# A two-layer attention and pooling trunk on one core: another order of column blocks, longer leads for weights, and w_ada's half tiles from the 33rd on issued by GpSimd

## The chip, the core and the metric

The kernel runs on one core of a Trainium2 chip. It is one program for five engines: TensorE (PE: matmuls and transposes; its weight loads are a row of their own, PEld), VectorE (DVE), ScalarE (ACT), GpSimd (POOL) and SyncE (SP). Here SP issues nearly all transfers between HBM and on-chip memory. Each engine carries out its instructions in the order in which the program wrote them, and each waits by itself for what its next instruction needs. The metric is the device time of one execution in microseconds (us), and less is better.

## The reference, cut to what matters

The sizes are a sequence of 256, a width of 2048 and 2 layers, all in float32. Each layer computes:

```python
mod = (c @ w_ada + b_ada)                        # w_ada: 2048 x 6144 per layer
shift, scale, gate = split(mod, 3)
h = rms_norm(x, g_pre) * (1 + scale) + shift
z = h @ w_in                                     # w_in: 2048 x 6144 per layer
u, g_pool, q, k, v, g_diff = split(z, 6)         # 1024 columns each
pool_out = multiscale_pool(u, w_pool, pool_scale) * silu(g_pool)
q, k = rope(q), rope(k)
att = rms_norm(diff_attention(q, k, v, lam), subln_g) * (1 - lam_init)
diff_out = att * silu(g_diff)
y = concat(pool_out, diff_out) @ w_out           # w_out: 2048 x 2048 per layer
x = x + (1 + gate) * rms_norm(y, g_post)
```

The kernel reads each weight once: w_ada (96 MB in 2^20 bytes for both layers), w_in (96 MB) and w_out (32 MB).

## The kernel before

**Weights.** `w_in` and `w_out` come in units of two k-tiles by 512 columns: 128 x 1024 float32 elements, 512 KB, one DMA, a tile named `rawz`. PE multiplies them in split form: ACT rounds a unit to `whiz` (function `cast`), and DVE subtracts that from the unit to get the remainder `wloz` (function `rest`). For each k-tile and each half of the sequence PE then does three products, high by high, high by low and low by high. The left side is split in the same way: `hz` tiles for `w_in` and `catz` tiles for `w_out`, each with a high and a low half.

**Blocks.** `w_in` has 12 column blocks of 512, two each for u (0, 1), g_pool (2, 3), q (4, 5), k (6, 7), v (8, 9) and g_diff (10, 11). `ORDERS` gives for each layer the order in which the blocks come to their end. A block whose sums are not whole when PE leaves it is copied out of PSUM to a `zz` tile and back in later (`accc<-zz`). When both blocks that a branch needs are done, a task for it starts: `pool_group` for a group of the pooling branch, `heads` for two attention heads. Each ends with a `catz` tile, which PE multiplies with `w_out`; four PE transposes of the gated result (`psb<-consts,zz`) stand ahead of a `catz` tile of the attention branch.

**w_ada.** The product with the vector c is not PE's work. `w_ada` is loaded transposed in half tiles of 128 x 1024 elements (512 KB, tiles named `adaz`), 192 in all and listed in `self.adas` in the order of use. DVE multiplies each by the spread c and sums along the row in one instruction, into one column of `mod`. From two `mod` columns come shift and scale of one k-tile (`AB`), and these make `hz`: ACT (or DVE) scales x by its norm into `halfz`, PE transposes that into PSUM (`psb<-consts,halfz`), ACT applies scale and shift. The last 32 columns of a layer give the gate. `RATE` says how many half tiles are placed in the plan per unit of weights, by layer and phase: (1, 2) is layer 1's gate tiles beside `w_in`.

**What sets the order.** Nothing reorders at run time. While the program is built, some fifty tasks ask for instructions, and a planner with a cost table (`Flow`) takes for each engine the most urgent one that could start. Urgency is a due time in PE's planned time: `need(u, before)` is the planned start of PE's use of unit u, less `before` us. So a larger `before` puts an instruction earlier among the others:

```python
    def need(self, u, before=0.0):
        return lambda: max(self.f.now["tensor"], self.f.time) + self.cum[u.step] - self.cum[self.at] - before
```

The change touches these due times: `load` (the DMA of a unit, 9.0 us ahead), `prepare` (an accumulator made ready, 3.5), `ada_due` (the multiplication of a half tile of w_ada, 6.0 us plus 1.3 for each half tile that must follow it; its load is due 4 us before that), and the last part of `pool_group` (3.0).

**Buffers.** 42 slots of 4 KB per partition in on-chip memory (`Slots`) hold all these tiles, `rawz`, `whiz`, `wloz`, `adaz`, `hz`, `catz`, `zz` and the temporary `halfz`. A new tile takes a slot that was given back, and its first instruction waits on its engine until the last user of that slot is done. A load that SP issues waits the same way, and all that SP issues later stands behind it. Eight PSUM banks hold sums and transposes.

All engine instructions go through one helper (`Watched.call`), so every row of the profile has that helper's line, L125; rows are told apart by the names of their tiles.

Of the kernel before, what the change touches and what calls it, by code (L numbers as in the profile page):

```python
# [22 lines left out]
D = 2048  # L23
# [381 lines left out]
class Kern:  # L405
# [31 lines left out]
    WARM = 18  # L437

    TURN = [3, 8]
    RATE = {(0, 2): 0.82, (1, 2): 0.85, (0, 0): 0.92, (0, 1): 0.9, (1, 0): 0.8, (1, 1): 0.35}  # L440
    ORDERS = [[10, 2, 3, 11, 6, 4, 0, 1, 7, 5, 8, 9], [2, 10, 11, 0, 6, 3, 4, 1, 7, 5, 8, 9]]

    HALVES = ((0, 4), (4, 8))

    def plan(self):
# [16 lines left out]
        def earn(rate):  # L462
            nonlocal credit
            credit = min(credit + rate, 2)
            while credit >= 1 and extras:
                take()
                credit -= 1
# [3 lines left out]
        for l in range(DEPTH):  # L471
            done, ended, first = [0] * 12, [], len(units)
            kp_at[l] = [None if t is None or (l == 0 and units) else 0 for t in kp_at[l]]
            while len(ended) < 12:
                for b in range(12):
# [7 lines left out]
                    for kp in range(done[b], av):  # L483
# [3 lines left out]
                        if not (l and len(units) <= first + 4):  # L487
                            earn(self.RATE[l, 2 if extras and extras[0][1] >= 32 else 0])
                    done[b] = av
                    if av == 8:  # L490
                        ended.append(b)
            block = dict(zip(ended, self.ORDERS[l]))
            for u in units:
                if u.w == "w_in" and u.l == l:
                    u.nb = block[u.nb]
            for n, nb in enumerate((0, 1, 2, 3, 2, 3, 0, 1)):
                late = n >= 4
                k0, k1 = self.HALVES[late]
                for kp in range(k0, k1):
# [5 lines left out]
                    if n < 6:  # L505
                        earn(self.RATE[l, 1])
            while l + 1 < DEPTH and kp_at[l + 1][self.START[l + 1] - 1] is None:
# [326 lines left out]
    def ada_due(self, e):  # L834
        l, nt, i = e
        if e in self.adas[:8]:
            return [-81.0, -6.0, -6.0, -6.0, -4.0, -4.0, -4.0, -4.0][self.adas.index(e)]
        if nt >= 32:
            return self.need(self.first_end[l]["w_out"], 15.0 + 1.3 * (2 * (48 - nt) - i))
        kt = nt % 16  # L840
        left = 4 * (kt % 2 == 0) + 2 * (nt < 16) + 1 - i
        return self.need_h(l, kt // 2, 6.0 + 1.3 * left)

    def load_ada(self):

# [6 lines left out]
    def ada_tile(self, e):  # L852
        l, nt, i = e
        w = self.big.take([P, D // 2], "ada", kind="ada", keep=4)
        self.nc.sync.dma_start(w, self.a["w_ada"][l, nt][:, i * D // 2 : (i + 1) * D // 2])
        self.ada_tiles[e] = w

    def ada(self):
# [169 lines left out]
    def load(self):  # L1028

        for u in self.units[self.count :]:  # L1030
            self.f.due(self.need(u, 9.0))
            raw = self.big.take([P, 2, NB], "raw", kind="raw", keep=4)
            self.nc.sync.dma_start(raw, self.a[u.w][u.l, u.nb][:, u.k : u.k + 2, :])
            u.raw = raw

    def cast(self):

        self.f.wait(lambda: len(self.h_whole) == 2 * NST)
        for u in self.units[self.count :]:
            self.f.due(self.need(u, 3.0))  # L1040
            self.f.wait(lambda: u.raw is not None)
            self.f.wait(lambda: self.big.count.get("hi", 0) - self.big.count.get("lo", 0) < 4)
            hi = self.big.take([P, 2, NB], "whi", F32R, kind="hi", keep=3)
            self.nc.scalar.copy(hi, u.raw)
            u.hi = hi
# [11 lines left out]
    def prepare(self):  # L1057

        turn = [v for v in self.visits if self.units[v.at].group == 3]
        for v in self.visits:  # L1060
            u = self.units[v.at]
            todo = [(w, st) for st in range(NST) for w in turn] if v is turn[0] else [] if v in turn else [(v, st) for st in range(NST)]
            for w, st in todo:
                self.f.due(self.need(self.units[w.at], 3.5 - st - (1.36 * u.count if w in turn and st else 0)))
                wide = u.group == 1 and [x for x in self.visits if self.units[x.at].group == 1].index(v) > 1
                acc = (self.banks if wide else self.accs).take([P, NB], "acc")
                if w.more:
                    src = (self.z if w.w == "w_in" else self.y)[w.l, w.nb]
                    self.f.wait(lambda: (w.w, w.l, w.nb, st) in self.saved)
                    self.copy(acc, src[:, st, :])  # L1070
                w.acc[st], w.ready[st] = acc, True
# [172 lines left out]
    def heads(self, l, hp):  # L1244

        nc, v, f = self.nc, self.nc.vector, self.f
# [8 lines left out]
        left = [2]  # L1255
# [50 lines left out]
        self.tmp.give(*aT)  # L1306
        self.drop(l, V[blk])
        self.pairs -= 1
        f.due(self.need_cat(l, 4 + hp, 8.0))
        ss = sm[:, 28:32]  # L1310
        for i in range(4):
            nc.scalar.activation(
# [8 lines left out]
        for i in range(4):  # L1321
            h, t = i // 2, i % 2
            g = gz[:, t, (h0 + h) * P : (h0 + h + 1) * P]
# [19 lines left out]
    def pool_group(self, l, g):  # L1343

        nc, f = self.nc, self.f
        half, gg = g // 2, g % 2
        u, gp = self.z[l, U[half]], self.z[l, GP[half]]
        f.wait(lambda: self.band is not None and self.wps[l] is not None)
        b = self.bank()
        for ct in range(2):  # L1350
            c = slice((2 * gg + ct) * P, (2 * gg + ct + 1) * P)
            o = b[:, ct * S : (ct + 1) * S]
            bd = self.band[:, g, :]

            nc.tensor.matmul(o[:, 0 : P + 16], u[:, 0, c], bd[:, 0 : P + 16], start=True, stop=False, skip_group_check=True)
            nc.tensor.matmul(o[:, P:S], u[:, 1, c], bd[:, P + 16 :], start=False, stop=True, skip_group_check=True)
        self.drop(l, U[half])
        pt = self.tmp.take([P, 2, S], "pt")
        self.copy(pt.rearrange("p c s -> p (c s)"), b)
        self.banks.give(b)  # L1360
        m = self.bank()
        for dt in range(2):
            for ct in range(2):
                nc.tensor.matmul(
                    m[:, dt * S : (dt + 1) * S], self.wps[l][half][:, 2 * gg + ct, dt * P : (dt + 1) * P], pt[:, ct, :],
                    start=ct == 0, stop=ct == 1,
                )
        self.tmp.give(pt)
        self.mixed[l] += 1
        if self.mixed[l] == 4:  # L1370
            self.big.give(*self.wps[l])
        for dt in range(2):
            zz = gp[:, gg, dt * S : (dt + 1) * S]
            nc.vector.scalar_tensor_tensor(
                zz, m[:, dt * S : (dt + 1) * S], self.cols[:, l, 80 + 2 * g + dt : 81 + 2 * g + dt], zz, op0=ALU.mult, op1=ALU.mult
            )
        self.banks.give(m)
        f.due(self.need_cat(l, g, 3.0))
        cat, hi, lo = self.two("cat")
        src = gp[:, gg, :].rearrange("p (d s) -> p d s", d=2)  # L1380
        nc.scalar.copy(hi, src)
        nc.vector.tensor_tensor(lo, src, hi.bitcast(F32), op=ALU.subtract)
        self.drop(l, GP[half])
        self.cat[l, g] = cat, hi, lo
# [98 lines left out]
```

## Time and profile before

| | us |
|---|---|
| three timed runs | 820.82, 821.57, 824.35 (median 821.57) |
| the profiled execution | 822.77, of which 821.0 is the span that the trace shows |
| PE busy (4032 instructions) | 796.9 of the span (97%) |
| DVE busy (1223) | 693.3 (84%) |
| ACT busy (980) | 549.7 (67%) |
| POOL busy (4) | 0.2 (0%) |
| moved by DMA | 245.06 MB (10^6 bytes), a mean of 299 GB/s |
| mean granted PE clock | 0.994 of full speed |

How to read it: "busy" is the time in which an engine carries out an instruction, and an idle stretch is put down to the instruction or the transfer of another engine that ended it, its releaser. A matmul is in flight for longer than the distance to the next one, so a high share of busy PE does not say that no time is lost: the gaps between starts do. The chain of waits is followed back from the last instruction, at each step to what released it, and "SPq" rows are waits of SP's own queue for a buffer.

### The profile page before, as it was taken

The numbers are of one execution on the slowest core, as the hardware profiler recorded it, in microseconds if no ns is written. First come the engines' busy times: TensorE is split into PE (matmuls) and PEld (weight loads), VectorE is DVE, ScalarE is ACT, GpSimd is POOL, SyncE is SP. The second block draws the span as 40 slices with busy tenths as digits, with TensorE's granted clock in tenths as the row PEclk, the third lists the DMA queues.
The fourth block names the chain that finished last, engine by engine and source line by source line (L and its number), as shares of the span: only waits on it lengthen the run. The fifth ranks groups of instructions, "written<-read, shape, count | busy, mean of one in ns | idle before, by whom it ended". The sixth has DMA issues, their size and how long they took to land.

```text
span 821.0 us, 11817 instructions
## 1 busy us (share of the span) xinstructions
PE 796.9 (97%) x4032; PEld 657.0 (80%) x4032; DVE 693.3 (84%) x1223; ACT 549.7 (67%) x980; POOL 0.2 (0%) x4
## 2 busy tenths in 40 slices
PE   7899999999999999999999999999999999999995
PEld 3588789888998888787878888788898887778884
DVE  6988999998889999799999888878789898878814
ACT  4779999876655667786488565666646557788521
POOL 0000000000000000000000000000000000000000
PEclk9999999999999999999999999999999999999998
DMA  9999997999998768877799699999899984555303
GB/s 342 406 409 409 408 402 246 387 370 365 358 376 334 259 202 290 306 253 254 264 352 338 233 370 333 318 369 366 322 393 363 344 300 130 185 176 179 126 0 102
DMA packets 68382, 245.06 MB, mean 299 GB/s; under 512 B 7745, under 2 KB 8033, under 8 KB 68065
## 3 DMA queue, kind: packets, MB, share of 16 engines
q1 hardware_dynamic: 68034, 244.14, 81.8%
q8 instruction: 31, 0.51, 0.2%
q10 hardware_dynamic: 288, 0.17, 0.1%
q14 instruction: 29, 0.24, 0.1%
HBM read 242.17 MB, written 2.11 MB: 298 GB/s over the span
## 4 chain that ended last, share of the span: by engine, by line
PE 84%; DMA 9%; DVE 3%; ACT 2%; issue 1%; SPq 0%; DVEq 0%; ACTq 0%
PE accc L125 76%; PE psb L125 8%; DMA adaz<-in_w_ada 5%; DMA rawz<-in_w_in 4%; DVE wloz L125 1%; DVE adaz L125 1%; ACT whiz L125 1%; DVE zz L125 0%; ACT zz L125 0%; ACT halfz L125 0%; DVE rh L125 0%; SPq L125 0%; DVE x L125 0%; DVE ry L125 0%; ACT accc L125 0%
## 5 line engine op out<-in xcount | busy, mean ns | idle before, releaser
L125 PE MATMUL accc<-whiz,hz 128*128 128x512 f32 x1256 | 397.1, 394 | 2.5 <-DVE hz L125 1.4
L125 ACT CAST whiz<-rawz 128x1024 fp32r<-128x1024 f32 x253 | 260.0, 1053 | 104.7 <-DMA rawz<-in_w_in 47.0
L125 DVE TENSOR_TENSOR wloz<-rawz,whiz 128x1024 fp32r<-128x1024 f32 x253 | 303.5, 1219 | 20.6 <-ACT whiz L125 19.5
L125 PEld LDWEIGHTS accc<-whiz,hz 128*128 128x128 f32 x1256 | 234.3, 188 | 54.3 <-DVE hz L125 2.7
L125 DVE SCALAR_TENSOR_TENSOR adaz<-adaz,cb 128x1024 f32<-128x1024 f32 x192 | 231.7, 1220 | 34.2 <-DMA adaz<-in_w_ada 33.1
L125 PE MATMUL accc<-wloz,hz 128*128 128x512 f32 x628 | 247.0, 393 | 0.9 <-DVE wloz L125 0.8
L125 PE MATMUL accc<-whiz,catz 128*128 128x512 f32 x512 | 164.9, 397 | 1.1 <-DVE catz L125 0.9
L125 PEld LDWEIGHTS accc<-wloz,hz 128*128 128x128 f32 x628 | 118.0, 188 | 27.0 <-DVE wloz L125 2.2
L125 PEld LDWEIGHTS accc<-whiz,catz 128*128 128x128 f32 x512 | 95.5, 188 | 22.4 <-DVE catz L125 1.8
L125 PE MATMUL accc<-wloz,catz 128*128 128x512 f32 x256 | 101.8, 398 | 0.0
L125 ACT COPY zz<-accc 128x512 f32<-128x512 f32 x128 | 74.2, 585 | 25.2 <-PE accc L125 24.4
L125 ACT COPY accc<-zz 128x512 f32<-128x512 f32 x109 | 64.4, 592 | 24.6 <-DVE halfz L125 17.8
L125 PE MATMUL accc<-hz,whiz 128*128 128x256 f32 x512 | 72.5, 283 | 0.0
L125 PEld LDWEIGHTS accc<-hz,whiz 128*128 128x128 f32 x512 | 66.8, 192 | 0.7
L125 PEld LDWEIGHTS accc<-wloz,catz 128*128 128x128 f32 x256 | 48.1, 188 | 10.2 <-issue 1.0
L125 PE MATMUL accc<-hz,wloz 128*128 128x256 f32 x256 | 41.1, 283 | 0.0
L125 PE MATMUL psb<-consts,halfz 128*128 128x128 f32 x176 | 31.0, 276 | 5.2 <-ACT halfz L125 5.2
L125 DVE TENSOR_TENSOR yz<-accc,Gz 128x512 f32<-128x512 f32 x16 | 11.0, 690 | 29.2 <-ACT sqj L125 29.0
L125 PEld LDWEIGHTS accc<-hz,wloz 128*128 128x128 f32 x256 | 35.3, 192 | 0.0
L125 PEld LDWEIGHTS psb<-consts,halfz 128*128 128x128 f32 x176 | 22.3, 140 | 14.8 <-ACT halfz L125 8.2
L125 ACT ACTIVATE sqj<-accc 128x512 bf16<-128x512 f32 x16 | 9.6, 599 | 36.1 <-PE accc L125 35.9
L125 ACT ACTIVATE halfz<-psb,sm 128x128 f32<-128x128 f32 x64 | 26.3, 421 | 2.4 <-DVE sm L125 0.9
(112 smaller groups left out, 510.4 us busy)
## 6 DMA issues: line engine op xcount, KB each, us to landing
adaz<-in_w_ada SPq DMA_DIRECT2D x192, 512.0 KB, 7.1
rawz<-in_w_in SPq DMA_DIRECT2D x189, 512.0 KB, 7.3
rawz<-in_w_out SPq DMA_DIRECT2D x64, 512.0 KB, 4.6
x<-in_x SPq DMA_DIRECT2D x2, 1024.0 KB, 9.0
wpz<-in_w_pool SPq DMA_DIRECT2D x4, 512.0 KB, 7.8
Gz<-gate SPq DMA_DIRECT2D x4, 512.0 KB, 5.5
out<-x SPq DMA_DIRECT2D x8, 256.0 KB, 2.8
rawz<-in_w_in SPq DMA_DIRECT2D x6, 256.0 KB, 8.8
```

What stands on the lines that cost most here:

```text
L125: return f(*args, **kw)
```

## The change

Four things change. The order in which the column blocks end is another in both layers. Due times lie earlier: w_ada's multiplications, and with them their loads, by 3 us, the loads of weights by 1, accumulators by 0.5 and the last part of `pool_group` by 1 (`cast` and `heads` stay at 3 and 8). The gate tiles of layer 1 are placed at a rate of 0.75 per unit instead of 0.85. And w_ada's half tiles from the 33rd on (160 of 192) are issued by GpSimd; the first 32 stay on SP.

```diff
-    RATE = {(0, 2): 0.82, (1, 2): 0.85, (0, 0): 0.92, (0, 1): 0.9, (1, 0): 0.8, (1, 1): 0.35}
-    ORDERS = [[10, 2, 3, 11, 6, 4, 0, 1, 7, 5, 8, 9], [2, 10, 11, 0, 6, 3, 4, 1, 7, 5, 8, 9]]
+    RATE = {(0, 2): 0.82, (1, 2): 0.75, (0, 0): 0.92, (0, 1): 0.9, (1, 0): 0.8, (1, 1): 0.35}
+    ORDERS = [[10, 2, 3, 11, 6, 4, 0, 1, 7, 8, 5, 9], [2, 10, 0, 6, 11, 3, 4, 8, 5, 1, 7, 9]]
...
-        return self.need_h(l, kt // 2, 6.0 + 1.3 * left)
+        return self.need_h(l, kt // 2, 9 + 1.3 * left)
...
-        self.nc.sync.dma_start(w, self.a["w_ada"][l, nt][:, i * D // 2 : (i + 1) * D // 2])
+
+        (self.nc.sync if self.adas.index(e) < 32 else self.nc.gpsimd).dma_start(w, self.a["w_ada"][l, nt][:, i * D // 2 : (i + 1) * D // 2])
...
-            self.f.due(self.need(u, 9.0))
+            self.f.due(self.need(u, 10))
...
-                self.f.due(self.need(self.units[w.at], 3.5 - st - (1.36 * u.count if w in turn and st else 0)))
+                self.f.due(self.need(self.units[w.at], 4 - st - (1.36 * u.count if w in turn and st else 0)))
...
-        f.due(self.need_cat(l, g, 3.0))
+        f.due(self.need_cat(l, g, 4))
```

The built programs hold the same instructions in another order; only 160 loads stand on another queue. Three places show what that means. In these rows the number in a tile's name tells its instance, and it differs between the two programs for the same piece of work.

The first place is SP's queue some 490 us into the execution, at the end of layer 0, while the weights of layer 1 begin to come. Before, SP issues loads of `w_in` (`rawz`) and of `w_ada` (`adaz`) in turn:

```order
L125 DMA rawz_4819<-in_w_in 128x1024
L125 DMA adaz_4826<-in_w_ada 128x1024
L125 DMA rawz_4834<-in_w_in 128x1024
L125 DMA adaz_4854<-in_w_ada 128x1024
L125 DMA rawz_4870<-in_w_in 128x1024
L125 DMA adaz_4884<-in_w_ada 128x1024
L125 DMA rawz_4903<-in_w_in 128x1024
L125 DMA adaz_4916<-in_w_ada 128x1024
```

After, SP's queue at that place holds weights alone:

```order
L125 DMA rawz_4774<-in_w_in 128x1024
L125 DMA rawz_4803<-in_w_in 128x1024
L125 DMA rawz_4823<-in_w_in 128x1024
L125 DMA rawz_4845<-in_w_in 128x1024
L125 DMA rawz_4868<-in_w_in 128x1024
```

And on POOL's queue, which held no load before, the half tiles of w_ada stand alone:

```order
L125 DMA adaz_4795<-in_w_ada 128x1024
L125 DMA adaz_4810<-in_w_ada 128x1024
L125 DMA adaz_4831<-in_w_ada 128x1024
L125 DMA adaz_4834<-in_w_ada 128x1024
L125 DMA adaz_4888<-in_w_ada 128x1024
```

The loads of w_ada have moved to a queue of their own, and a load of weights no longer has one of them ahead of it.

The second place is DVE's queue shortly after that, ahead of the first `hz` tiles of layer 1. Here w_ada's multiplications (SCALAR_TENSOR_TENSOR), the splits of weights (`wloz`) and the small sums for shift and scale (`AB`) stand in one line. The scaled x of layer 1, `halfz_4965` on ACT, goes into the buffer of rawz_4870 and waits until `wloz_4934` has read it. Before:

```order
L125 SCALAR_TENSOR_TENSOR adaz_4826,mod_89<-adaz_4826,cb_78 128x1024
L125 TENSOR_TENSOR wloz_4893<-rawz_4819,whiz_4890 128x1024
L125 SCALAR_TENSOR_TENSOR adaz_4854,mod_89<-adaz_4854,cb_78 128x1024
L125 TENSOR_TENSOR wloz_4902<-rawz_4834,whiz_4892 128x1024
L125 TENSOR_TENSOR AB_91<-mod_89 128x2x2
L125 TENSOR_TENSOR wloz_4934<-rawz_4870,whiz_4926 128x1024
L125 TENSOR_TENSOR AB_91<-AB_91,b_107 128x2x2
L125 TENSOR_TENSOR AB_91<-AB_91,cols_84 128x2
L125 SCALAR_TENSOR_TENSOR adaz_4884,mod_89<-adaz_4884,cb_78 128x1024
```

After, the scaled x is `halfz_4956`, and it goes into the buffer of rawz_4845, which `wloz_4924` frees:

```order
L125 SCALAR_TENSOR_TENSOR adaz_4810,mod_89<-adaz_4810,cb_78 128x1024
L125 TENSOR_TENSOR wloz_4858<-rawz_4803,whiz_4856 128x1024
L125 SCALAR_TENSOR_TENSOR adaz_4831,mod_89<-adaz_4831,cb_78 128x1024
L125 SCALAR_TENSOR_TENSOR adaz_4834,mod_89<-adaz_4834,cb_78 128x1024
L125 TENSOR_TENSOR wloz_4898<-rawz_4823,whiz_4895 128x1024
L125 TENSOR_TENSOR AB_91<-mod_89 128x2x2
L125 TENSOR_TENSOR AB_91<-AB_91,b_107 128x2x2
L125 TENSOR_TENSOR wloz_4924<-rawz_4845,whiz_4897 128x1024
L125 TENSOR_TENSOR AB_91<-AB_91,cols_84 128x2
L125 TENSOR_TENSOR wloz_4943<-rawz_4868,whiz_4931 128x1024
```

Two multiplications of w_ada now follow each other ahead of the splits, and one more split stands behind the one that frees the buffer.

The third place is PE's queue in `w_out` of layer 0, at one tile of the attention branch (the wait at 378.12 us of the execution before). The last of four transposes into a PSUM bank is the first row here; ACT and DVE make `catz_3753` from that bank, and the last row is its first use. Before:

```order
L125 MATMUL psb_3754<-consts_80,zz_511 128x128
L125 MATMUL accc_3257<-whiz_3417,catz_3655 128x512
L125 MATMUL accc_3252<-whiz_3417,catz_3655 128x512
L125 MATMUL accc_3252<-wloz_3441,catz_3655 128x512
L125 MATMUL accc_3252<-whiz_3417,catz_3655 128x512
L125 MATMUL accc_3257<-whiz_3417,catz_3655 128x512
L125 MATMUL accc_3257<-wloz_3441,catz_3655 128x512
L125 MATMUL accc_3257<-whiz_3417,catz_3655 128x512
L125 MATMUL accc_3252<-whiz_3440,catz_3753 128x512
```

After, the same piece of work is `psb_3783` and `catz_3782`. The rows shown are the last two transposes, the end of the unit that was running, and the start of the next unit; nine more matmuls of that unit with `catz_3746` follow, and then the first use of `catz_3782`:

```order
L125 MATMUL psb_3783<-consts_80,zz_507 128x128 x2
L125 MATMUL accc_3283<-whiz_3434,catz_3658 128x512
L125 MATMUL accc_3281<-whiz_3471,catz_3746 128x512
L125 MATMUL accc_3281<-wloz_3497,catz_3746 128x512
L125 MATMUL accc_3281<-whiz_3471,catz_3746 128x512
```

The transposes have moved ahead of a whole unit of other work: 13 matmuls stand between the last transpose and the tile's first use, where there were 7.

More of the change, by code (lines that the diff above doesn't have):

```diff
@@ L1039, in cast @@
         for u in self.units[self.count :]:
-            self.f.due(self.need(u, 3.0))
+            self.f.due(self.need(u, 3))
             self.f.wait(lambda: u.raw is not None)
@@ L1308, in heads @@
         self.pairs -= 1
-        f.due(self.need_cat(l, 4 + hp, 8.0))
+        f.due(self.need_cat(l, 4 + hp, 8))
         ss = sm[:, 28:32]
```

## The prediction

> **What bounds the kernel now.** I read the page's head first, then a table of three stretches, then the list of what TensorE (PE) waited for, then each of those waits in the timeline, and last the queue and the chain behind the longest of them.
>
> ```profile
> span 821.0 us, 11817 instructions
> PE 796.9 (97%) x4032; PEld 657.0 (80%) x4032; DVE 693.3 (84%) x1223; ACT 549.7 (67%) x980; POOL 0.2 (0%) x4
> 0.00:100.00 100.00, 90.67 (x391) 67.03 (x392) 85.77 (x169) 75.84 (x124) 0.20 (x4) 0.98 1.01 395
> 100.00:620.00 520.00, 515.27 (x2672) 434.02 (x2671) 462.08 (x767) 358.57 (x611) 0.00 (x0) 1.00 0.89 323
> 620.00:821.00 201.00, 190.92 (x973) 155.91 (x971) 145.49 (x289) 115.33 (x247) 0.00 (x0) 0.98 0.55 186
> 771.12 40.83 PE accc L125 x180
> ```
>
> The three rows of stretches give PE, weight loads, VectorE (DVE), ScalarE (ACT), GpSimd (POOL), then PE's granted clock, the DMA share and GB/s. PE is busy nearly everywhere at full clock, and DMA is full only in the first 100 us. The last row is a stretch of the chain in which nothing but matmuls stand: 40.83 us / 180 = 0.227 us from one 128x512 matmul to the next. So PE's work is a fixed line of matmuls, and time can only come out of its gaps. The change adds and removes no matmul.
>
> ```profile
> PE psb L125 <- ACT halfz L125: 5.2, 3, 2.9
> PE psb L125 <- DMA cb<-in_c: 2.8, 1, 2.8
> PE accc L125 <- ACT halfz L125: 2.6, 2, 2.0
> PE accc L125 <- DVE hz L125: 1.4, 2, 1.2
> PE accc L125 <- DVE catz L125: 0.9, 2, 0.5
> PE accc L125 <- ACT accc L125: 0.8, 2, 0.7
> PE accc L125 <- DVE wloz L125: 0.8, 1, 0.8
> PE accc L125 <- ACT hz L125: 0.3, 1, 0.3
> PE accc L125 <- DVE zz L125: 0.2, 1, 0.2
> ```
>
> These are all of PE's waits (total us, times, longest). Not one of them names a weight's DMA: PE waits for short chains on ACT and DVE. The same waits, one by one, with the idle time in brackets:
>
> ```profile
> 84.23 0.50 PE L125 MATMUL accc<-wloz,hz 128*128 128x512 f32 x1 [0.83 <-DVE wloz L125]
> 374.17 0.50 PE L125 MATMUL accc<-whiz,catz 128*128 128x512 f32 x1 [0.45 <-DVE catz L125]
> 378.12 0.50 PE L125 MATMUL accc<-whiz,catz 128*128 128x512 f32 x1 [0.45 <-DVE catz L125]
> 428.91 0.50 PE L125 MATMUL accc<-whiz,hz 128*128 128x512 f32 x1 [0.29 <-ACT hz L125]
> 430.86 0.50 PE L125 MATMUL accc<-whiz,hz 128*128 128x512 f32 x1 [1.21 <-DVE hz L125]
> 503.29 0.33 PE L125 MATMUL psb<-consts,halfz 128*128 128x128 f32 x1 [0.76 <-ACT halfz L125]
> 527.57 0.39 PE L125 MATMUL accc<-whiz,hz 128*128 128x512 f32 x1
> 529.50 0.33 PE L125 MATMUL psb<-consts,halfz 128*128 128x128 f32 x1 [1.55 <-ACT halfz L125]
> 703.66 0.50 PE L125 MATMUL accc<-whiz,hz 128*128 128x512 f32 x1 [0.67 <-ACT accc L125]
> 704.80 0.50 PE L125 MATMUL accc<-whiz,hz 128*128 128x512 f32 x1 [0.17 <-ACT accc L125]
> 707.32 0.50 PE L125 MATMUL accc<-whiz,catz 128*128 128x512 f32 x1 [0.17 <-DVE zz L125]
> ```
>
> The matmul at 527.57 lasts 0.39 us, but the next could have begun 0.227 us after its start: it began 1.93 us later, so 1.70 us are lost where the bracket says 1.55. I add 0.17 us to every bracket for that. After 100 us nine waits stand here, 5.72 us of brackets + 9 x 0.17 = 7.25 us. That is what this change can win in 720 us; the rest of the list lies in the first 90 us (the 0.83 at 84.23 with it), and the order of the first 30 us stays as it is.
>
> **Behind the longest waits** stands w_ada. The chain that ends at 503.29:
>
> ```profile
> 491.88 7.15 DMA adaz<-in_w_ada
> 500.29 0.10 DVE wloz L125
> 501.50 1.20 DVE wloz L125
> 502.73 0.52 ACT halfz L125
> 503.29 0.33 PE psb L125
> ```
>
> A half tile of w_ada takes 7.15 us to land, DVE stands still for it in order, the two splits of weights behind it come late, the second frees the buffer that ACT's scaled x goes into, and PE's transposes wait for that.
>
> **The change, part by part.** The profiled execution took 822.77 us (span 821.0 and 1.8 around it), 1.20 more than the median 821.57; I make the sum as a difference and take it from the median.
>
> ```profile
> SPq L125 <- PE accc L125: 221.3, 113, 12.6
> SPq L125 <- DVE adaz L125: 90.0, 52, 5.5
> L125 SPq DMA_DIRECT2D adaz<-in_w_ada x192: 327/328/1476, 2.0 to 668.1; - x192
> DMA to landing us min/median/max: 3.1/7.1/10.8
> L125 DVE SCALAR_TENSOR_TENSOR adaz<-adaz,cb 128x1024 f32<-128x1024 f32 x192 | 231.7, 1220 | 34.2 <-DMA adaz<-in_w_ada 33.1
> ```
>
> *160 of w_ada's 192 loads leave SP's queue for POOL's, each with its waits.* SP held its next load for a buffer that PE (221.3 us) or DVE (90.0 us) still used, so a tile of w_ada kept weights behind it waiting and the other way round. An issue costs SP 0.33 us, 52 us for 160, while SP mostly waits: worth 0 on the path. On POOL's queue stand only these loads (the page gives POOL 0.2 us of work), so a waiting one holds back no other kind; who waits for it is DVE's multiplication. No row shows a load that POOL issues. Its landing is bounded by SP's own 3.1 and 10.8 us, from 4.0 us earlier to 3.7 us later than the median 7.1. I take 1 us later, nearer to the median because the 16 DMA engines and the bytes stay the same; it is covered by the next edit. If the cover goes, DVE is late.
>
> *More lead.* w_ada is due 9 instead of 6 us ahead, so an arrival up to 3 us later costs DVE no more than now. The weights' 9 to 10 and the accumulators' 3.5 to 4 act in the same direction: by themselves 0. What they can cost is in the first 100 us, where DMA is full: a half tile of 0.524 MB at 395 GB/s is 1.33 us, so two tiles let ahead of a weight make +2.7, and the wait at 84.23 gone makes 0.83 + 0.17 = -1.0. I take 0, since the first 32 half tiles remain on SP among the same weights.
>
> *The places of the scaled x in layer 1 (503.29 and 529.50).* Loss now 0.76 + 1.55 + 0.34 = 2.65 us. In the new order the buffer is freed by the last split but one (wloz_4924, with wloz_4943 behind it) instead of the last (wloz_4934), one split and so about 1.2 us (the 1.20 of the chain) sooner, and the w_ada tiles ahead of it come over a queue in which no weight stands. I take all of it, -2.65; bounds 0 (still late) and -2.65.
>
> *The cat tiles of layer 0 (374.17 and 378.12).* Loss 0.90 + 0.34 = 1.24. PE had 7 matmuls, 7 x 0.227 = 1.6 us, between the last transpose and the tile's first use; the new order has 13, 2.9 us. The wait was 0.62 each, so 2.2 us would do: -1.24; bounds 0 and -1.24.
>
> *The layer boundary (428.91 and 430.86).* Loss 0.29 + 1.21 + 0.34 = 1.84. The next layer's first h needs the finished x of this one, whichever blocks come later; only DVE gets freer. Bounds 0 and -1.84; half, -0.92.
>
> *The copies at 703.66 to 707.32.* Loss 1.01 + 0.51 = 1.52. Here ACT copies a sum out, a sum in, and PE waits. The block whose partial sums are turned here is another now, the copies are as many. Bounds 0 and -1.52; half, -0.76.
>
> *Waits that the new order makes.* Nearly every row after the first 30 us moves, so new near misses are likely. Bounds 0 and the 7.25 that the old order has; I take one of the size of a cat wait, +0.62, because the whole list has only nine.
>
> *RATE 0.85 to 0.75* spreads the last layer's gate tiles, whose last load SP issued at 668.1; they are needed at its output's end, when the matmuls of 771.12 run: 0, covered by those 100 us.
>
> Sum: -2.65 - 1.24 - 0.92 - 0.76 + 0.62 = -4.95. 821.57 - 4.95 = 816.6 us (817.8 for an execution like the profiled one).
>
> **The rivals.** *No measurable change, 821 us.* The loads are as many, the buffers are as many, and SP waits for buffers and not for its own issuing: then w_ada, asked for earlier, takes buffers from the weights, the waits of layer 1 (2.65 and 0.92) come back and the new waits cancel the rest (821.57 - 1.24 - 0.76 + 2 x 0.62 = 820.8). For it: the 221.3 us on PE's releases. Against it: PE never waited for a weight's landing. The Trainium skill's page "DMA: Bandwidth & Descriptors", section "Issuing engines are not separate DMA queues", says that loads from several engines run on the same 16 DMA engines and that a second issuer saves only the issuing time; by that rule, too, the result is about 821. The trace agrees that issuing is cheap (0.33 us), but a queue that waits in order is not in that rule.
>
> *Slower, 838 us: POOL's loads land late.* DVE multiplies in order, so each late tile holds up the splits behind it. Lateness is free up to the 3 us of lead; after that DVE's idle time in 100 to 620 us, 520 - 462.08 = 57.9 us, absorbs 57.9 / 160 = 0.36 us a tile. From 3.4 us later DVE sets the pace; at 3.5, 160 x 0.5 - 57.9 = 22 us come on top of 816.6. For it: DVE is at 89% there and has waited 33.1 us for w_ada already, and nothing shows POOL's loads. Against it: it takes POOL's typical load to be as slow as SP's slowest.
>
> ```profile
> L125 DVE COPY accc<-zz 128x512 f32<-128x512 f32 x17 | 11.7, 691 | 4.5 <-ACT zz L125 4.4
> ```
>
> The Trainium skill's page "SBUF — State Buffer" warns in "SBUF: two separate sides" that loads issued by GpSimd starve while VectorE copies float32 within SBUF at its doubled rate, with 3.1 us for a load that takes 0.62 alone; by that the lateness would be some 2.5 us, an estimate from the page's figures, still within the lead. What DVE copies here goes to or from PSUM, 0.69 us for 512 columns, so the rule's case hardly occurs in these rows.
>
> **Chances and range.** Gain as summed 0.60 (own range 812.5 to 819), no change 0.27, slower 0.13. The range's low end is every wait after 100 us and the one at 84.23 gone, 821.57 - 7.25 - 1.0 = 813.3, less the 0.8 by which the fastest run lies under the median: 812.5. The high end is no change with two tiles in the way early, 821.57 + 2.7 = 824.3, so 824.5; that leaves out 0.12 above and some 0.04 below. A change of 0.5%, 4.1 us, is about what a measurement can tell from none: faster means under 817.5, and 816.6 lies close to it, so 0.55 faster, 0.33 the same, 0.12 slower.
>
> **What would show it.** Right: POOL shows 160 loads; PE's waits for halfz and catz after 100 us are gone; DVE's idle time for w_ada is no more than 33.1 us; the cast and split of weights run earlier against PE. Wrong: a landing of w_ada above 10 us, DVE near 95% between 100 and 620 us, or PE waits of over 2 us at places that the list doesn't have now. The forecast fails most easily at the half shares (0.92 and 0.76) and at the new waits, for which no row of before has a price.

## The result, and the profile after

The changed kernel is slower. Its six runs took 823.43 to 841.82 us, median 833.62; the kernel before took 819.30 to 824.35 in as many runs, median 821.32. The ratio is 1.0123 (95% interval 1.0083 to 1.0163); this and every ratio below leaves out runs that lie more than 1.5% above the fastest of the same kernel (here two of the changed one), so it can be a little under the ratio of the medians (here 1.015). The runs spread by 18 us where those of before spread by 5. The forecast was 816.6 us with a range of 812.5 to 824.5.

The profiled execution took 838.52 us. The head of its page, and the same three stretches as before (engines in the same order, then PE's granted clock, the DMA share and GB/s):

```profile
span 836.7 us, 11846 instructions
PE 800.8 (96%) x4032; PEld 663.5 (79%) x4032; DVE 697.1 (83%) x1232; ACT 545.4 (65%) x971; POOL 84.8 (10%) x164
0.00:100.00 100.00, 91.04 (x400) 68.98 (x401) 89.46 (x174) 78.32 (x128) 3.50 (x10) 1.00 1.00 395
100.00:620.00 520.00, 507.61 (x2619) 427.75 (x2618) 450.51 (x757) 346.07 (x591) 71.29 (x135) 0.99 0.88 315
620.00:836.70 216.70, 202.18 (x1017) 166.73 (x1015) 157.17 (x303) 121.05 (x254) 10.02 (x19) 0.98 0.56 194
```

The section on the change says that the two programs hold the same instructions. The counts show a small difference: nine more of the copies and scalings run on DVE instead of ACT (DVE 1232 where it had 1223, ACT 971 where it had 980). PE has the same 4032.

No engine has become the bound. DVE's busy share between 100 and 620 us has fallen from 89% to 87%, and PE has 12.4 us without a matmul there where it had 4.7. What PE waited for, in the list of all its waits:

```profile
PE psb L125 <- ACT halfz L125: 11.0, 4, 3.1
PE psb L125 <- DVE halfz L125: 4.8, 4, 1.6
PE psb L125 <- ACT zz L125: 3.1, 1, 3.1
PE psb L125 <- DMA cb<-in_c: 2.8, 1, 2.8
PE accc L125 <- ACT halfz L125: 2.2, 2, 1.7
PE accc L125 <- ACT zz L125: 1.3, 2, 0.7
PE accc L125 <- DVE wloz L125: 0.9, 1, 0.9
PE accc L125 <- ACT accc L125: 0.8, 1, 0.8
PE accc L125 <- DVE hz L125: 0.6, 2, 0.4
```

Still no weight's transfer is named, and the waits for `catz` are gone. But the sum is 27.5 us where it was 15.0, and single waits after 100 us now reach 3 us, where the longest was 1.55. DVE's own wait for tiles of w_ada, 33.1 us before (42 times, longest 2.4), has grown too:

```profile
DVE adaz L125 <- DMA adaz<-in_w_ada: 49.3, 37, 4.4
```

The loads themselves do not look worse at their middle. The rows for the tiles of w_ada, first POOL's issues (shortest, median and longest, in ns), then the landing of all of them:

```profile
L125 POOL DMA_DIRECT2D adaz<-in_w_ada x160: 527/530/664, 85.8 to 688.1; - x160
DMA to landing us min/median/max: 4.0/7.7/13.4
```

The same landing row for the tiles of weights (`rawz`), after:

```profile
DMA to landing us min/median/max: 3.5/7.0/18.8
```

and before:

```profile
DMA to landing us min/median/max: 3.4/6.7/11.6
```

The medians moved by 0.3 us for weights and from 7.1 to 7.7 for w_ada. The ends moved: the slowest weight lands 18.8 us after its issue instead of 11.6. From the issue and landing times of the loads of w_in, w_out and w_ada after 85 us, as far as the trace tells their landing, comes a second difference: before, none of 336 loads landed ahead of one issued earlier; after, 46 of 356 were overtaken. In 50 of the 67 pairs it is a weight of SP's queue that is passed by a tile of w_ada issued later on POOL's, by a median of 2.2 us and at most 9.0. A second profiled execution of the same kernel, 830.90 us long, shows the same: 39 of 356 overtaken, the slowest weight 19.6 us after its issue.

**One of the long waits.** These are DVE's rows ahead of the first scaled x of layer 1, the second place of the order shown above (the rows of accumulators left out):

```profile
495.09 1.23 DVE L125 SCALAR_TENSOR_TENSOR adaz<-adaz,cb 128x1024 f32<-128x1024 f32 x1 [3.48 <-DMA adaz<-in_w_ada]
496.24 1.22 DVE L125 TENSOR_TENSOR wloz<-rawz,whiz 128x1024 fp32r<-128x1024 f32 x1
497.97 1.23 DVE L125 SCALAR_TENSOR_TENSOR adaz<-adaz,cb 128x1024 f32<-128x1024 f32 x1 [0.50 <-DMA adaz<-in_w_ada]
...
506.01 1.23 DVE L125 SCALAR_TENSOR_TENSOR adaz<-adaz,cb 128x1024 f32<-128x1024 f32 x1 [1.30 <-DMA adaz<-in_w_ada]
507.17 1.22 DVE L125 TENSOR_TENSOR wloz<-rawz,whiz 128x1024 fp32r<-128x1024 f32 x1
...
508.57 1.23 DVE L125 TENSOR_TENSOR wloz<-rawz,whiz 128x1024 fp32r<-128x1024 f32 x1
```

ACT's scaled x behind it, and PE's transposes behind that:

```profile
509.83 0.91 ACT L125 ACTIVATE halfz<-x,ry 128x256 f32<-128x256 f32 x2 [2.60 <-DVE wloz L125]
510.39 0.47 PE L125 MATMUL psb<-consts,halfz 128*128 128x128 f32 x1 [3.10 <-ACT halfz L125]
```

DVE waits five times for w_ada's tiles in the 14.4 us up to 506.01 (the three waits shown, and 0.59 and 0.18 in rows left out), 6.05 us in all, and does everything else in between, in order. The chain is the one shown of before (a tile of w_ada, a split, the scaled x, PE), only longer: 3.10 us instead of 0.76. In the second profiled execution PE waited 2.02 us there.

**What a gap costs beyond itself.** The granted clock (third number from the end) in the microseconds around that gap:

```profile
508.00:509.00 1.00, 0.00 (x0) 0.00 (x0) 0.96 (x4) 0.00 (x0) 0.00 (x0) 1.00 0.99 377
509.00:510.00 1.00, 0.00 (x0) 0.00 (x0) 1.00 (x3) 0.17 (x1) 0.00 (x0) 0.61 0.97 365
510.00:511.00 1.00, 0.60 (x3) 0.61 (x4) 1.00 (x2) 0.74 (x2) 0.00 (x0) 0.50 1.03 377
...
515.00:516.00 1.00, 1.00 (x4) 0.81 (x3) 1.00 (x3) 0.96 (x3) 0.53 (x1) 0.50 0.01 4
516.00:517.00 1.00, 1.00 (x5) 0.82 (x5) 1.00 (x3) 1.00 (x3) 0.00 (x0) 0.98 0.53 160
```

PE ran at half its clock for 6.8 us, which loses up to another 3.4. It happened again after the gaps at 645 and 693 us, for 3.4 us each; the profiled execution of before has one such stretch of 3.4 us, at 26 us. Take the time from each matmul's start to the next one's, and what of it lies above the usual for its kind (the median over both traces for the same tiles and shapes). The sum is 38.9 us before and 54.1 after, and the difference, 15.2, is nearly all of the 15.7 us by which the span grew. Half clock makes at most 6.8 against 1.7 of it, some 5; the rest, some 10, are the gaps.

### The profile page after: what moved, and what is told of

It reads as the page before. It is cut to its first block, busy times and chain, and to the rows that moved or that the text cites. A ratio compares the mean times of both kernels' runs of the same rounds, so it can differ in the third digit from the quotient of the medians.

```text
span 836.7 us, 11846 instructions
## 1 busy us (share of the span) xinstructions
PE 800.8 (96%) x4032; PEld 663.5 (79%) x4032; DVE 697.1 (83%) x1232; ACT 545.4 (65%) x971; POOL 84.8 (10%) x164
## 5 line engine op out<-in xcount | busy, mean ns | idle before, releaser
L125 DVE SCALAR_TENSOR_TENSOR adaz<-adaz,cb 128x1024 f32<-128x1024 f32 x192 | 231.3, 1219 | 49.9 <-DMA adaz<-in_w_ada 49.3
L125 POOL DMA_DIRECT2D adaz<-in_w_ada x160 | 84.6, 530 | 603.6 <-DVE wloz L125 181.6
L125 ACT COPY zz<-accc 128x512 f32<-128x512 f32 x121 | 69.7, 585 | 10.7 <-PE accc L125 10.4
L125 PE MATMUL accc<-hz,wloz 128*128 128x256 f32 x256 | 42.9, 288 | 0.0
```

The lines of the kernel that those rows point to most:

```text
L125: return f(*args, **kw)
```

## The experiments

**Which part of the change does it.** The planner keeps its own account of SP and POOL, so putting a load on another queue also changes the order of everything else. The helper can be split in two: an issue that the planner counts for one queue while the chip issues it from the other. Then two kernels have the same rows on PE, DVE and ACT and differ in the queue alone.

The changed kernel with all loads of w_ada on SP, in plan and in fact:

```diff
-        (self.nc.sync if self.adas.index(e) < 32 else self.nc.gpsimd).dma_start(w, ...)
+        self.nc.sync.dma_start(w, ...)
```

> The changed kernel with all 192 half tiles of w_ada issued by SP again, and planned so; new block orders, rate and leads stay. Theory A (the second queue does the harm: loads of w_ada on POOL share the DMA engines with SP's weights and land out of the order in which DVE and ACT need them): the loss is gone, 815 to 822 us, runs within 3 us of each other, PE's gaps after 100 us at most 7 us. Theory B (the new order and the longer leads do the harm, because earlier w_ada takes buffers from the weights): 828 us or more. Theory C (planner: a kernel planned with two queues is ordered worse): 815 to 822, as A.

Measured: 817.76 us (815.15 to 819.68, 12 runs), ratio to the kernel before 0.9968 (0.9955 to 0.9981). The loss is gone and 2.9 us are won. Theory B falls. The runs spread by 4.5 us, a little more than theory A's 3.

The same built order, with the 160 half tiles issued by POOL:

```diff
+        self.ada_queue = Watched(self, "sync", nc.gpsimd)
...
+        (self.nc.sync if self.adas.index(e) < 32 else self.nc.ada_queue).dma_start(w, ...)
```

> The same built order of every engine as the kernel with all half tiles on SP, but the 160 half tiles from the 33rd on are issued by POOL: only the queue differs. Theory A: as slow and as irregular as the changed kernel, 828 to 840 us, with PE gaps of over 2 us and stretches at a granted clock of 0.5. Theory B: the same as the kernel with all on SP, whatever that is, within 3 us. Theory C: the same as the kernel with all on SP, within 3 us, and that one fast.

Measured: 834.15 us (825.84 to 838.97), ratio 1.0176 (1.0140 to 1.0213). By the queue alone 16.4 us are lost, and the runs are irregular again. Set against PE's progress (both kernels start the same matmuls in the same order), the loads land as before at the median (w_ada 0.07 us later, weights 0.02 earlier), but a tenth of w_ada's tiles from the 33rd on land over 1.7 us earlier and a tenth over 2.0 later; for all weights it is 2.0 and 2.1.

The reverse, the order of the changed kernel with every load issued by SP (`Watched(self, "gpsimd", nc.sync)`):

> The built order of the changed kernel on PE, DVE and ACT, but every load of w_ada is issued by SP, in the planner's order: only the queue differs from the changed kernel. Theory A: 815 to 823 us, the gaps of over 2 us after 100 us gone. Theory B: 828 us or more. Theory C (the planner's order is what is bad): 828 us or more, with gaps at the same instructions as in the changed kernel.

Measured: 818.10 us (813.66 to 821.45, 12 runs), ratio 0.9968 (0.9950 to 0.9986). The planner's order was not bad, so theory C falls too. At the place shown above this kernel's DVE waited at most 1.54 us for a tile of w_ada, and its PE row is:

```profile
498.69 0.33 PE L125 MATMUL psb<-consts,halfz 128*128 128x128 f32 x1 [0.19 <-ACT halfz L125]
```

The same instruction, behind the same rows, waits 0.19 us on one queue and 3.10 on two.

And the kernel before, its order untouched, with the 160 half tiles issued by POOL:

> The kernel before with its own order of every engine, in which the half tiles of w_ada from the 33rd on are issued by POOL: only the queue differs from the kernel before. Theory A: slower than the kernel before, by 6 to 20 us, and irregular from run to run. Theories B and C: 820 to 823 us, no difference.

Measured: 841.41 us (835.53 to 849.46), ratio 1.0246 (1.0215 to 1.0277): 20.7 us lost, a little over theory A's 20. In three pairs, then, the second queue cost 15.5, 16.4 and 20.7 us by the medians (1.6, 2.1 and 2.5% by the ratios); without it the rest of the change wins 2.9. In all three the profiled executions show no load overtaken with one queue (of 336) and 33 to 46 of 356 with two, and at most 7 loads in flight with one and 11 with two. DVE's wait for tiles of w_ada goes from 34.4 to 49.3, 34.8 to 40.8 and 33.1 to 50.2 us.

One could think that the loads come late only because they are issued at other times. The traces of the three pairs tell the two apart. The weights of `w_in` that land over 2 us later against PE's progress are issued within 0.2 us of the same point at the median, and are 2.3 to 3.5 us longer in flight. So it is the flight that got longer for them. The late tiles of w_ada are both issued later (1.3 to 2.2 us at the median) and longer in flight (0.8 to 1.7).

**The queues by themselves.**

> No trunk is computed here: the kernel only copies x to the output and loads 128 half tiles of w_ada (512 KB each) in eight groups of 16, and each group starts when VectorE is through with the one before. Who issues: SP alone; SP and POOL in turn; SP and ACT in turn; POOL alone; then the four once more. Theory A1 (any second queue shares the DMA engines, so loads in flight on two queues land together and out of their order): in the groups with one queue the loads land one by one, about 1.3 us apart, in order; in both kinds of mixed groups a load takes longer on the one queue while the other's go ahead, and loads overtake by a microsecond or more. Theory A2 (it is POOL's way to issue that is slow): in the group of POOL alone the loads land further apart or the first lands over 1 us later than with SP alone, and the group of SP and ACT is as orderly as SP alone.

VectorE reads one element per partition of each tile in turn, so its waits show the landings. SP alone (first group, its first four tiles):

```profile
19.74 0.15 DVE L65 COPY junk__76<-t__60 128x1 f32<-128x1 f32 x1 [19.74 <-DMA t__60<-in_w_ada]
20.97 0.15 DVE L65 COPY junk__76<-t__61 128x1 f32<-128x1 f32 x1 [1.08 <-DMA t__61<-in_w_ada]
22.24 0.15 DVE L65 COPY junk__76<-t__62 128x1 f32<-128x1 f32 x1 [1.11 <-DMA t__62<-in_w_ada]
23.53 0.15 DVE L65 COPY junk__76<-t__63 128x1 f32<-128x1 f32 x1 [1.14 <-DMA t__63<-in_w_ada]
```

One tile each 1.28 us, in order. SP and POOL in turn (even tiles on SP, odd ones on POOL; the group starts at 39.04):

```profile
43.63 0.15 DVE L65 COPY junk__76<-t__60 128x1 f32<-128x1 f32 x1 [4.33 <-DMA t__60<-in_w_ada]
48.55 0.15 DVE L65 COPY junk__76<-t__61 128x1 f32<-128x1 f32 x1 [4.77 <-DMA t__61<-in_w_ada]
48.66 0.15 DVE L65 COPY junk__76<-t__62 128x1 f32<-128x1 f32 x1
51.11 0.15 DVE L65 COPY junk__76<-t__63 128x1 f32<-128x1 f32 x1 [2.30 <-DMA t__63<-in_w_ada]
51.22 0.15 DVE L65 COPY junk__76<-t__64 128x1 f32<-128x1 f32 x1
```

SP's tiles land at 4.5, 7.2, 10.1 and 12.6 us from the group's start and POOL's at 9.4, 12.0, 14.5 and 17.1: each queue now gets a tile every 2.56 us, half the rate, and POOL's first comes 4.9 us after SP's although it was issued 0.3 us later. When the group is repeated it is 3.9 us. A reader that takes them in order stands still for 4.77 us. POOL alone is as quick as SP alone:

```profile
92.16 0.15 DVE L65 COPY junk__76<-t__60 128x1 f32<-128x1 f32 x1 [4.12 <-DMA t__60<-in_w_ada]
93.39 0.15 DVE L65 COPY junk__76<-t__61 128x1 f32<-128x1 f32 x1 [1.07 <-DMA t__61<-in_w_ada]
```

Its first tile lands 4.1 us after the group's start (SP alone, repeated: 3.9) and later ones mostly 1.28 apart. SP and ACT in turn also share, but land in pairs 0.2 to 0.5 us apart and in order. All kinds of group take 22.8 to 25.7 us for 16 tiles, so nothing is lost of the rate. Theory A1 holds in its core, the sharing, but its overtaking is not common to any two queues: it came with POOL's late start beside SP, which neither theory had. Theory A2 falls as it was put. Here it is SP's loads that pass POOL's. In the trunk it is mostly a tile on POOL's queue that passes a weight on SP's, so POOL's late start does not explain most of the overtaking there.

**The order and the leads, on one queue.** The kernel before with the new `ORDERS` and `RATE` alone:

> The kernel before with the new block orders and the rate 0.75; leads as before, all loads on SP. The gain of the changed order and leads on one queue was 0.3%. If the order makes it: 816 to 819 us, and the waits for the scaled x of layer 1 (0.9 and 1.7 us of PE) smaller or gone. If the leads make it: 820 to 822 us.

Measured: 818.34 us (816.34 to 821.13, 12 runs), ratio 0.9983 (0.9966 to 0.9999).

The kernel before with the longer leads alone:

> The kernel before with the longer leads (w_ada 9, weights 10, accumulators 4, pool groups 4); block orders and rate as before, all loads on SP. If the leads make the gain of 0.3%: 816 to 819 us. If the order makes it: 820 to 822 us. If more lead only takes buffers from the weights: over 822 us.

Measured: 822.66 us (820.43 to 827.23, 12 runs), ratio 1.0032 (1.0012 to 1.0052). The order by itself makes about 2.0 us of the gain, barely clear of noise; the leads by themselves cost 2.3. That is what was expected if more lead only takes buffers from the weights, but why they cost wasn't followed further.

**Half the dose.** POOL issues from the 113th half tile on (`< 112` for `< 32`):

> The changed kernel, but only the half tiles from the 113th on (80 instead of 160) are issued by POOL. Theory A (each load on the second queue makes trouble by itself): the loss against the kernel with all on SP (817.8) falls to about half of 16 us, so 822 to 830 us, and PE has no new gap before the 113th half tile. A rival, that the loss comes from a single place (one long wait in layer 0 with what follows from it): the whole loss or none, so over 832 or under 820 us.

Measured: 824.76 us (815.28 to 830.98, 12 runs), ratio 1.0028 (1.0001 to 1.0055). Against the kernel with all on SP (817.76) that is 7.0 us for 80 loads, where 160 cost 15.9 (833.62): about in proportion. The rival of a single place falls by the median. The runs, though, go from no loss to 13 us. The profiled execution is the fastest of them, 815.28 us: 15 of 346 loads were overtaken in it, by up to 4.0 us, and after the first 30 us PE has one distance of over 1.5 us from one matmul's start to the next (1.82, at 629 us; POOL's first load is at 400). So loads that land out of order need not cost anything. That they cost only where the one that needs them has no slack left would fit, but is not shown.

**Can lead cover it?** The changed kernel with the leads of before:

> The changed kernel (new block orders, rate 0.75, 160 half tiles on POOL) with the leads of before: w_ada 6, weights 9, accumulators 3.5, pool groups 3. If longer leads cover part of the disorder that the second queue makes: slower than the changed kernel (833.6), 836 to 842 us, since the kernel before with POOL took 841.4. If the leads do nothing there: 830 to 836 us. If they do harm on two queues as they do on one (822.7 against 820.3): 826 to 832 us.

Measured: 830.54 us (827.67 to 837.97), which fits both "do nothing" and "do harm"; that longer leads help is not borne out. With 3 us more lead again (w_ada 12, weights 13):

> The changed kernel with 3 us more lead again (w_ada 12, weights 13), loads on two queues. If lead alone can cover the disorder, whose spread of landings against PE's progress was about 2 us either way: 820 to 828 us. If buffers set the time of the loads, so that asking earlier changes no landing: 830 to 838 us.

Measured: 830.53 us (826.77 to 835.94). All loads on SP, w_ada's lead back at 6:

> All loads on SP, new block orders and rate, weights 10, accumulators 4, pool groups 4 as in the changed kernel, but w_ada's lead back at 6. The leads alone cost 2.3 us on one queue and the order alone won 2.0. If w_ada's lead is what costs (its tiles hold buffers that the weights need): 814 to 817 us, below the 817.8 with all leads long. If the order decides and the leads do nothing beside it: 817 to 819 us.

Measured: 818.42 us (817.53 to 822.73, 12 runs), ratio 0.9989 (0.9972 to 1.0006); that w_ada's lead is what costs is not borne out, and its difference from the kernel before is not clear of noise. And the changed kernel beside them:

> The changed kernel once more, unchanged, beside the other three: 826 to 842 us, and again spread by 10 us or more between runs, because PE's gaps come and go with the order in which two queues' loads land and because a gap costs 3.4 or 6.8 us at half clock in some runs and nothing in others.

Measured: 832.35 us (822.48 to 836.34), ratio 1.0107 (1.0063 to 1.0151). On two queues three settings of the lead give 830.5, 832.4 and 830.5 us, within the spread of their runs: asking earlier does not help. A load waits for a buffer before it is issued (in the first profiled execution POOL waited 181.6 us for splits, 85.3 of them ahead of its first load, and 175.5 for matmuls), so the due time alone does not set its landing.

The second profiled execution of the unchanged kernel also shows the clock's part in the spread. At the layer boundary the first execution had a wait of 2.89 us and kept its clock:

```profile
421.56 0.44 PE L125 MATMUL psb<-consts,halfz 128*128 128x128 f32 x2 [2.89 <-ACT halfz L125]
```

```profile
422.00:423.00 1.00, 1.00 (x6) 0.78 (x6) 0.90 (x6) 1.00 (x3) 0.66 (x2) 1.00 1.03 422
```

The second had the same wait at 2.00 us, and half the clock for 3.4 us behind it:

```profile
420.42 0.69 PE L125 MATMUL psb<-consts,halfz 128*128 128x128 f32 x2 [2.00 <-ACT halfz L125]
```

```profile
421.00:422.00 1.00, 1.00 (x4) 0.81 (x4) 0.93 (x4) 1.00 (x4) 0.80 (x2) 0.50 1.02 414
```

## Why the prediction was wrong, point by point

**The step that failed** is "160 of w_ada's 192 loads leave SP's queue for POOL's". It was costed at 0: a landing 1 us later, covered by 3 us more lead. It cost 15.5 to 20.7 us. The typical landing was not badly sized: in the three pairs the median landing of w_ada's tiles from the 33rd on moves by 0.2 to 0.3 us, less than the 1 us taken. What was wrong was to price a load by its median latency, to price only the loads that moved, and to take SP's queue as mere obstruction. The bounds from SP's rows did not hold on two queues, where the slowest tile of w_ada takes 13.4 us and not 10.8. The weights that stayed on SP had no term at all, and their slowest landing went from 11.6 to 18.8. SP's one line was also what kept the loads landing in the order in which they are needed. On two queues a weight asked for earlier shares the DMA engines with w_ada's tile asked for later (two queues at once each got half the rate, and late weights were 2.3 to 3.5 us longer in flight), and the order of need is lost by some 2 us either way. That it is mostly weights that are passed fits equal shares per queue, since SP's is the longer line here; this reading was not tested by itself. DVE and ACT take their tiles in order, so early tiles win nothing and late ones hold up all behind them.

**The cover** ("by the next edit") failed as well. Three leads gave the same time on two queues.

**The rival "slower, 838 us"** had the right sign and nearly the size, but its mechanism is not what happened. It wanted POOL's typical load 3.5 us late and DVE near 95% between 100 and 620 us; the median is 0.6 us later and DVE fell to 87%. Its chance of 0.13 was set by a threshold on typical lateness, and the loss comes from the tail. Of the signs in the list of what would show it, "PE waits of over 2 us at places that the list doesn't have now" did appear (2.14 at 202 us, 3.13 at 648), and DVE's idle time for w_ada went to 49.3 us, over the 33.1 that was the limit for being right. "A landing of w_ada above 10 us" could tell nothing, since the kernel before already had one of 10.8.

**The rival "no measurable change"** drew on the Trainium skill, page "DMA: Bandwidth & Descriptors", section "Issuing engines are not separate DMA queues". The rates agree with it: 16 tiles take 22.8 to 25.7 us whoever issues. The same section says that such loads interleave with each other. The prediction read this as neutral. Here it was not: the time between tiles went from 1.28 us on one queue to 2.56 on each of two, and the kernel lost 15 to 21 us. The other page weighed, "SBUF — State Buffer", section "SBUF: two separate sides", warned of starved issues by GpSimd; POOL's issue took 527 to 664 ns throughout, so no run here shows that.

**The gains** were mostly right, which shows on one queue. In the profiled execution with all on SP the waits for the scaled x of layer 1 are gone as summed (-2.65), the two waits for cat tiles of layer 0 are gone (-1.24), and the boundary's longest wait shrank from 1.21 to 0.41. The new order alone kept one wait for the scaled x (1.19) and both cat waits, so these came from order and leads together. The copies near 700 us did not gain: 0.87 to 0.89 us are lost there twice (at 674 and 693), where -0.76 was summed. New waits made 2.2 us in three gaps of 0.55 to 0.98, against +0.62. The sum without POOL's step was -4.95; the medians say -2.9.

**One reading was loose.** The chain at 503.29 was told as if DVE stood still for the tile that took 7.15 us. DVE waited under 0.1 us for that one; it had stood still for the three tiles ahead of it (0.87, 1.57 and 0.25 us). That w_ada made the splits late stands all the same.

**What the sum left out** is the clock. A gap was priced at its length. The stretch at 26 us in the trace of before already showed a gap of 2.6 us followed by 3.4 us at half clock, and it was read only as a mean of 0.98 over the first 100 us. The mean granted clock of the runs of the changed kernel has a median of 0.9905, that of 23 runs of the kernel before 0.995: 0.0095 x 833 = 7.9 us against 0.005 x 821 = 4.1, so some 4 of the 12 us.

## What to carry to other kernels

One queue that issues in the order of need is also what makes transfers land in that order; here a second queue took that away without adding any rate, so before moving loads off a busy queue ask who consumes them in order, and look at the longest landings, those of the loads that stay included, and not at the median alone. Price a wait of TensorE at more than its length where it may halve the clock. To learn what an edit to a planned kernel does, hold the built order fixed and change one thing in the chip's program alone. The version to keep here is the changed one with all loads on SP: 817.8 us, 0.3% under the kernel before.

## What the runs showed of the hardware

- The half clock comes in stretches of 3.4 or 6.8 us, and the length of a gap does not tell whether it brings one. The 1.61 us from one matmul to the next at the layer boundary brought one in the kernel before with POOL (427 us) and none in the kernel before (429 us). One of 2.39 us did, and 3.27 and 2.53 did not. The Trainium skill, page "TensorE: Matmul & The Clock Gate", section "Part 1: The HAM clock gate (the "warmup" mystery)", tells of a free-running window of 3413 ns; the lengths agree, and so does it that the same gap can end either way. It asks for an idle window of about 3.4 us, and here idle stretches that the rows give as 1.21 us (427 us, the kernel before with POOL) and 2.00 us were enough, so the measurement decides.
- POOL's first load beside a busy SP queue landed 3.9 and 4.9 us after SP's, ACT's 0.3 and 0.5; alone POOL needed no longer than SP. What holds it back no run here shows, nor how much of the loss is due to that and how much to sharing; a trunk with w_ada on ACT's queue wasn't tried, since ACT would stand still at each wait for a buffer.
